# Fused decoder layer on one core: the first six hidden tiles' down projection as seven products for eight, their block sums by GpSimd, and a last plain chunk of four tiles

## The chip, the cores and the metric

The kernel runs on one core of one Trainium2 chip. The metric is the device time of one execution in microseconds. Engines are named as in the profile: PE (TensorE matmul), PEld (TensorE weight load), DVE (VectorE), ACT (ScalarE), POOL (GpSimd) and SP (SyncE, which issues most transfers). An index behind "L" is a line of the kernel before.

## The reference

The kernel computes one layer for 576 tokens (512 of a prompt, 64 of a sample group): a mixer, a cross attention and a feed-forward part. The change is in the feed-forward part and in the residual behind it:

```python
x = x + _rms(o) * g_post_x
u = _rms(x) * g_pre_ffn
f = (jax.nn.silu(u @ w_gate) * (u @ w_up)) @ w_down
x = x + _rms(f) * g_post_ffn
```

`x` is 576 x 1024, `w_gate` and `w_up` are 1024 x 2816, `w_down` is 2816 x 1024. The 2816 hidden features are 22 tiles of 128.

## The kernel before

**Layout and precision.** Everything lies with features on the partitions and the 576 tokens along the free axis. Each float32 operand is split into a high part (a cast to fp32r, by ACT) and a low part (the difference, mostly by DVE), and every product is three matmuls: high by high, high by low, low by high. `split` (L190, L191) is this pair of instructions. Tokens are cut in two in one of two ways: `HALVES` (256 and 320) for plain products, `E` (288 and 288) for the others.

**Gate and up.** Hidden tiles 0 to 3 are plain products (`half_tile`, L1693): eight input tiles by three matmuls for each half. `gated` (L1700) then applies silu (ACT, L1683) and the product with up (DVE, L1686) and writes the hidden tile's high and low parts with `hidden` (L1688) to the buffers `hh` and `hl`. Tiles 4 to 21 go in pairs, in class `Pair` (L1853), which computes a 2 x 2 block product with seven block products in place of eight. For that it needs sums and differences of the weights' blocks (`sums`, `diffs`, `parts2` to `parts4` of class `Seven`, on ACT, DVE and by accumulating transfers that POOL issues) and of the activations' blocks (`tsum`). A pair runs in three stretches. `early` has products 0 and 1, `mid` 2, 3 and 4, `late` 5 and 6. Product 2 accumulates into the same bank as product 0 (`s.x`), so it waits until ACT has copied that bank to `cc` (L1881); product 4 in turn waits until ACT has copied it to `ct` (`ev2`, L1888), and product 5 until the copy to `cc` (`ev3`, L1892). One pair's `late` is run behind the next one's `early`.

**Down.** Before, the down projection has four chunks of hidden tiles:

- tiles 0 to 3, plain (`down_chunk`, L1998, from L2066), right behind the first pair; ACT copies the results to `f2`;
- tiles 4 to 9 and 10 to 15, seven products for eight (class `Down`, L1939); DVE adds each product to `f2` (L1947). They read block sums of the hidden tiles, which `Hidden.sums` (L1928, DVE) computes from a pair's four gated blocks in `gt` before these are overwritten;
- tiles 16 to 21, plain: first the 320 tokens for all eight output tiles (L2112), then the 256 tokens, in the tail.

**The tail** (from L2117) is written out by hand: `half0` are the products of 256 tokens, `evac0` adds a bank to `f2`, squares it and scales it by the gain, `sum0` adds up the squares, `resid1` finishes the 320 tokens (norm, residual, store), `x_rows` and `x_copy` turn the residual's tiles around, and `f_rows`, `root` and `last` finish the 256 tokens.

**Order.** From L2037 on, for tiles 0 to 3 and the first pair (`pp[0]` for gate, `pp[1]` for up), and again in the tail, the order on every engine is that of a table of positions: `at_(p, step)` puts a step at position p, and the steps are traced in rising p. A unit of p is one half tile's 24 matmuls in the first table and one output tile's products in the second. In between, a scheduler orders each engine's instructions at build time. In either case every engine takes its instructions strictly in order.

Of the kernel before, what the change touches and what calls it, by code (L numbers as in the profile page):

```python
# [115 lines left out]
def build(nc, tc, ctx, I, O):  # L116
# [72 lines left out]
    def split(hi, lo, src, eng=None, cast=None):  # L189
        c = (cast or A.copy)(hi, src)  # L190
        (eng or V).tensor_tensor(lo, src, hi.bitcast(F32), op=ALU.subtract)  # L191
        return c
# [843 lines left out]
    def SL0(name, dt=F32R):  # L1036
        return big0.tile([P, KT, T], dt, name=name, tag="s0", bufs=1)
# [639 lines left out]
    at_(12.9, S.dma_start, x_d, x)  # L1677


    H = []  # L1680

    def silu(j, i):
        A.activation(ct[:, (j + i) % 2, :], B[("g", j), i], AF.Silu)  # L1683
# [2 lines left out]
        V.tensor_tensor(ct[:, (j + i) % 2, :], ct[:, (j + i) % 2, :], B[("u", j), i], op=ALU.mult)  # L1686

    def hidden(j, i):  # L1688
        if not H:
            H.extend((SL0("hh0"), SL(2, "hl0", F32R)))  # L1690
        split(H[0][:, j, E[i]], H[1][:, j, E[i]], ct[:, (j + i) % 2, :])

    def half_tile(*ms):  # L1693

# [208 lines left out]
    class Hidden:  # L1903
# [90 lines left out]
    def down_part(nk, j, i, ps, w, k0, k1):  # L1994
        t0, n = HALVES[i]
        return gemm(ps, [(*w, nk)], act(hh), act(hl), t0, n, k0, k1)

    def down_chunk(nk, order, last, w_of, evac, n1):  # L1998

        ps = {}  # L2000

        def get(j, i):
            if (j, i) not in ps:
                ps[j, i] = (GP if len(ps) < 3 or len(ps) % 2 else MP)("ps_dn")[:, :HALVES[i][1]]
            return ps[j, i]

        for n_, (j, i) in enumerate(order[:3]):
            down_part(nk, j, i, get(j, i), w_of(j), 0, n1)
            if n_ == 0:
                last.late()  # L2010
        for n_, (j, i) in enumerate(order):
            p = get(j, i)
            m = down_part(nk, j, i, p, w_of(j), n1 if n_ < 3 else 0, nk) if n_ > 2 or n1 < nk else None
            evac(n_, j, i, p, m)

    def ev_first(n_, j, i, ps, m):
        t0, n = HALVES[i]
# [12 lines left out]
    for p, n_, step in ((19.05, 0, "load"), (19.1, 1, "load"), (21.9, 0, "sums"), (22.05, 0, "high1"), (22.6, 0, "diffs"),  # L2030
                        (23.0, 0, "place3"), (23.05, 0, "parts2"), (23.9, 1, "sums"), (24.1, 0, "parts3"),
                        (23.62, 0, "parts4"), (24.48, 0, "early"), (24.97, 1, "high1"), (25.0, 0, "mid"),
                        (25.4, 1, "diffs"), (26.05, 1, "parts2"), (26.48, 1, "early"), (27.5, 0, "late"),
                        (26.45, 1, "place3"), (26.47, 1, "parts4"), (28.1, 1, "parts3"), (28.5, 1, "mid")):
        at_(p, lambda n_, step: getattr(pp[n_], step)(), n_, step)
    plan.sort()
    with tc.manual_schedule(engines={TE.engine, A.engine, V.engine, G.engine, S.engine}):  # L2037
        for p, _, fn in plan:
# [10 lines left out]
        for p, _, fn in plan:  # L2049
            if p > 19.02:  # L2050
                fn()
    hh, hl = H
    f2 = SL(4, "f_ffn")


    firsts = {}

    def w_first(j):
        if j not in firsts:
            with tc.issue_after(pp[0].ev3.ins) if j < 2 else ExitStack():  # L2060
# [12 lines left out]
    class Plain:  # L2073
# [1 line left out]
            s.b = hh, hl  # L2075

        def put(s, j, a, i, g):
            split(*[t_[:, j % 8, E[i]] for t_ in s.b], g)


    for n_, j0 in enumerate((10, 16)):
        store = stores[-1]
        last = run([lambda: Pair(j0, 0, None)] + downs(512 + 768 * n_, store), last)
        stores.append((Plain if n_ else Hidden)(SL0("hh%d" % n_), SL(2, "hl%d" % n_, F32R)))
        last = run([pair(j0, 1, stores[-1])] + [pair(j, up, stores[-1]) for j in (j0 + 2, j0 + 4) for up in range(2)], last)
# [4 lines left out]
    wdh = SL(1, "wdh", F32R, (P, 6, 768))  # L2090
    wdl = bx.tile([P, 16, 288], F32R, name="wdl", tag="b5").rearrange("p a b -> p (a b)").rearrange("p (j c) -> p j c", c=768)
    x2 = SL(3, "x2")
    ssqf = ssq_tile("ssqf")
    rb = rb_tile("pf_rb")
# [1 line left out]

    def w_of(j):
        if j not in kept:
            src = I["wdown"][j, :, 2048:2816]
            raw = fp.tile([P, 1024], F32, name="rawx", tag="rawx", bufs=2) if j % 2 else None  # L2100
            kept[j] = split_w(src, 768, 768, raw=raw, to=None if j > 5 else (wdh[:, j, :], wdl[:, j, :]))
        return kept[j]

    def down_evac(n_, j, i, ps, m):
# [40 lines left out]
    def half0(j, k):  # L2145
        if k == 0:
            tail[j] = (MP if j % 2 else GP)("ps_dn")[:, :256]
        down_part(6, j, 0, tail[j], w_of(j), k, k + 1)

    def evac0(j):  # L2150
        fj = f2[:, j, 0:256]
        V.tensor_tensor(fj, fj, tail[j], op=ALU.add)
# [10 lines left out]

    def resid1(q):
        o, c = f2[:, 2 * q:2 * q + 2, 256:T], x2[:, 2 * q:2 * q + 2, 256:T]
        V.tensor_tensor(o, o, rb[:, 256:T].unsqueeze(1).to_broadcast([P, 2, 320]), op=ALU.mult)
        V.tensor_tensor(c, c, o, op=ALU.add)
        S.dma_start(O["y1"][:, 2 * q:2 * q + 2, :], c)

    for j in range(8):  # L2170
        for k in range(6):
            at_(j + k / 6, half0, j, k)
        at_(j + 1.03, evac0, j)
        if 0 < j < 7:
            at_(j + 1.45, sum0, j)
    at_(0.99, root, "pf1", [(ssqf, 0)], HCHUNKS[1])
    at_(1.9, root_end, "pf1")
    at_(2.32, root_rows1)
    at_(2.6, lambda: A.copy(rb[:, 256:T], tail["ps"][:, 0:320]))
    for q, p in enumerate((2.95, 4.1, 5.1, 6.1)):  # L2180
        at_(p, resid1, q)

    parts = [(c, d) for c in range(2) for d in range(2)]
# [38 lines left out]
        store(3)  # L2222

    for i in range(4):
        at_(4.0 + i, x_rows, i)
        at_(4.55 + i, x_copy, i)
# [40 lines left out]
def pack(inp):  # L2267
# [37 lines left out]
    out["wup"] = _units(i["w_up"][0], KT)  # L2305

    w = _units(i["w_down"][0], NFFN)
    taken = [0, 1, 2, 3] + [j + k for j in (4, 10) for k in (0, 2, 4, 1, 3, 5)] + list(range(16, 22))
# [47 lines left out]
```

## Time and profile before

| | |
|---|---|
| median of 3 runs | 1096.13 us (1095.41 to 1097.32) |
| the profiled execution | 1096.77 us, span 1095.0 us |
| granted TensorE clock, mean | 0.998 |
| busy share of the span | PE 99%, PEld 94%, DVE 69%, ACT 56%, POOL 21% |
| matmuls | 8124 |
| bytes moved | 182.29 MB, mean 166 GB/s |

All traces are of the profiled execution; what lies around its span is 1.77 us. A row of a timeline has the start, the length, the engine, the line, the operation, the tile written and the tiles read, and the shape; in brackets stands the idle time before it and what ended it. Rows of PE overlap (matmuls are pipelined), so the price of a matmul is the distance from one start to the next.

### The profile page before, as it was taken

The numbers are of one execution on the slowest core, as the hardware profiler recorded it, in microseconds if no ns is written. First come the engines' busy times: TensorE is split into PE (matmuls) and PEld (weight loads), VectorE is DVE, ScalarE is ACT, GpSimd is POOL, SyncE is SP. The second block draws the span as 40 slices with busy tenths as digits, with TensorE's granted clock in tenths as the row PEclk, the third lists the DMA queues.
The fourth block names the chain that finished last, engine by engine and source line by source line (L and its number), as shares of the span: only waits on it lengthen the run. The fifth ranks groups of instructions, "written<-read, shape, count | busy, mean of one in ns | idle before, by whom it ended". The sixth has DMA issues, their size and how long they took to land.

```text
span 1095.0 us, 20715 instructions
## 1 busy us (share of the span) xinstructions
PE 1084.1 (99%) x8124; PEld 1027.5 (94%) x8124; DVE 754.0 (69%) x1507; ACT 611.7 (56%) x1098; POOL 225.8 (21%) x305
## 2 busy tenths in 40 slices
PE   9999999999999999999999999999999999999997
PEld 8999887778999999999988879999999999999997
DVE  6896785658877775558744546676566877787555
ACT  7767632455654555656545445645566566656653
POOL 1332643313213112000144301100011121111000
PEclk9999999999999999999999999999999999999999
DMA  6785635435655349653467775644386687588532
GB/s 204 170 154 127 170 111 174 163 84 177 189 149 146 106 132 312 205 189 102 150 215 271 264 248 163 217 161 109 104 195 142 150 196 173 116 188 186 128 130 88
DMA packets 58967, 182.29 MB, mean 166 GB/s; under 512 B 6605, under 2 KB 11853, under 8 KB 58357
## 3 DMA queue, kind: packets, MB, share of 16 engines
q1 hardware_dynamic: 42740, 138.06, 39.0%
q0 software_dynamic: 15552, 41.95, 19.8%
q8 instruction: 64, 1.05, 0.4%
q10 hardware_dynamic: 576, 0.95, 0.3%
q14 instruction: 35, 0.28, 0.1%
HBM read 160.28 MB, written 20.65 MB: 165 GB/s over the span
## 4 chain that ended last, share of the span: by engine, by line
PE 88%; DVE 5%; ACT 4%; DMA 2%; issue 1%; SPq 0%; POOL 0%; DVEq 0%; ACTq 0%
PE ps_v L814 5%; PE ps_in L202 4%; PE ps_in L201 4%; PE ps_in L204 4%; PE ps_o L202 3%; PE ps_o L204 3%; PE ps_o L201 3%; PE ps_g L1848 3%; PE ps_g L1849 3%; PE ps_g L1850 3%; PE ps_u L1848 3%; PE ps_u L1850 3%; PE ps_u L1849 3%; PE ps_dn L1848 2%; PE ps_dn L1849 2%; PE ps_dn L202 2%
## 5 line engine op out<-in xcount | busy, mean ns | idle before, releaser
L201 PE MATMUL ps_in<-uh,whi 128*128 128x320 f32 (+1 forms) x544 | 164.0, 302 | 0.4 <-DVE cb L450 0.4
L204 PE MATMUL ps_in<-uh,wlo 128*128 128x320 f32 (+1 forms) x544 | 163.2, 300 | 0.0
L202 PE MATMUL ps_in<-ul,whi 128*128 128x320 f32 (+1 forms) x544 | 162.7, 299 | 0.0
L179 ACT CAST whi<-raw 128x1024 fp32r<-128x1024 f32 (+1 forms) x104 | 105.2, 1013 | 96.2 <-PE ps_in L202 26.1
L186 DVE TENSOR_TENSOR wlo<-raw,whi 128x512 fp32r<-128x512 f32 (+1 forms) x96 | 96.6, 1009 | 66.5 <-ACT whi L179 65.8
L201 PEld LDWEIGHTS ps_in<-uh,whi 128*128 128x128 f32 x544 | 103.1, 190 | 3.4 <-issue 1.7
L204 PEld LDWEIGHTS ps_in<-uh,wlo 128*128 128x128 f32 x544 | 103.0, 190 | 1.2 <-issue 0.4
L202 PEld LDWEIGHTS ps_in<-ul,whi 128*128 128x128 f32 x544 | 103.1, 190 | 0.6
L184 POOL DMA_DIRECT2D wlo<-win x32 | 27.9, 871 | 80.1 <-ACT wlo L183 72.0
L1848 PE MATMUL ps_g<-b,whi 128*128 128x288 f32 x144 | 42.5, 295 | 0.0
L1849 PE MATMUL ps_g<-b,whi 128*128 128x288 f32 x144 | 42.4, 295 | 0.0
L1848 PE MATMUL ps_u<-b,whi 128*128 128x288 f32 x144 | 42.4, 295 | 0.0
L1849 PE MATMUL ps_u<-b,whi 128*128 128x288 f32 x144 | 42.4, 295 | 0.0
L1821 ACT CAST whi<-rawx 128x1024 fp32r<-128x1024 f32 (+1 forms) x26 | 25.7, 987 | 27.8 <-PE ps_dn L1849 13.8
L191 DVE TENSOR_TENSOR wlo<-sw,whi 128x1024 fp32r<-128x1024 f32 (+1 forms) x26 | 29.6, 1140 | 14.9 <-ACT whi L190 14.7
L201 PE MATMUL ps_xo<-qh,whi 128*128 128x288 f32 x128 | 38.5, 302 | 0.2 <-ACT whi L179 0.2
L202 PE MATMUL ps_o<-mixs_l,whi 128*128 128x320 f32 (+1 forms) x128 | 38.2, 299 | 0.0
L204 PE MATMUL ps_o<-mixm_h,wlo 128*128 128x256 f32 (+1 forms) x128 | 38.2, 298 | 0.0
L202 PE MATMUL ps_o<-mixm_l,whi 128*128 128x256 f32 (+1 forms) x128 | 37.9, 296 | 0.0
L201 PE MATMUL ps_xq<-u2h,whi 128*128 128x320 f32 (+1 forms) x128 | 37.9, 300 | 0.0
L201 PE MATMUL ps_o<-mixm_h,whi 128*128 128x256 f32 (+1 forms) x128 | 37.9, 296 | 0.0
L204 PE MATMUL ps_xq<-u2h,wlo 128*128 128x320 f32 (+1 forms) x128 | 37.9, 296 | 0.0
(765 smaller groups left out, 3838.9 us busy)
## 6 DMA issues: line engine op xcount, KB each, us to landing
raw<-win SPq DMA_DIRECT2D x35, 512.0 KB, 3.9
raw<-wout SPq DMA_DIRECT2D x17, 512.0 KB, 3.6
raw<-wxq SPq DMA_DIRECT2D x13, 512.0 KB, 3.6
raw<-wgate SPq DMA_DIRECT2D x13, 512.0 KB, 3.5
raw<-wup SPq DMA_DIRECT2D x13, 512.0 KB, 5.3
wlo<-win POOLq DMA_DIRECT2D x24, 256.0 KB, 5.1
kva<-kc SPq DMA_DIRECT2D x12, 512.0 KB, 5.7
kva<-vc SPq DMA_DIRECT2D x12, 512.0 KB, 6.0
```

The costliest lines, as they stand in the source:

```text
L179: casts.append(A.copy(hi[:, :n], raw[:, :n]))
L184: G.dma_start(lo[:, a:b], src[:, a:b], accum_op=ALU.add)
L186: e.tensor_tensor(lo[:, a:b], raw[:, a:b], hi[:, a:b].bitcast(F32), op=ALU.subtract)
L191: (eng or V).tensor_tensor(lo, src, hi.bitcast(F32), op=ALU.subtract)
L201: mm(ps, wh, ah, start=i == 0, stop=False)
L202: mm(ps, wh, al, start=False, stop=False)
L204: m = mm(ps, tiles[order[c]][1], xh(order[c], t0, n), start=False, stop=c == len(tiles) - 1)
L814: mm(ps, a, b, skip_group_check=True, **kw)
L1821: A.copy(s.h3[:, s.all], s.r2[:, s.all])
L1848: mm(ps, wh, b[0][k], start=start and k == 0, stop=False, skip_group_check=True)
L1849: mm(ps, wh, b[1][k], start=False, stop=False, skip_group_check=True)
L1850: m = mm(ps, wl, b[0][k], start=False, stop=k == nk - 1, skip_group_check=True)
```

## The change

Tiles 0 to 3 are no longer projected by themselves. The pairs' chunks become tiles 0 to 5, 6 to 11 and 12 to 17, all with `Down`, and the plain last chunk keeps tiles 18 to 21. The order of the tiles in the packed weight follows.

`Down` needs block sums of tiles 0 and 1, and of 2 and 3. The gated blocks of these tiles come one by one, and only their high and low parts are kept (the blocks that `Down` doesn't read go to `te`). So `single_sums` computes each pair's four sums out of the parts, with ten tensor-tensor instructions on POOL into `gt`, and `single_parts` splits them (a cast of 1152 columns on ACT, a difference on DVE). The positions of these four steps in the first table are new. In the first chunk, ACT copies a product to `f2` where it is the first one. The tail's positions are new, and in it POOL scales output tiles 0 to 5 and does one of the four residuals.

```diff
     def hidden(j, i):
-        split(H[0][:, j, E[i]], H[1][:, j, E[i]], ct[:, (j + i) % 2, :])
+        split(*stores[0].single(j, i), ct[:, (j + i) % 2, :])
...
+        def single(s, j, i):
+            if (j % 2, i) == (0, 1):
+                return [s.rest()[:, j + e, :] for e in range(2)]
+            return s.place(j // 2, {(0, 0): 4, (1, 0): 5, (1, 1): 6}[j % 2, i])
+
+        def single_sums(s, q):
+            g, b = gates(4 + 2 * q), [[[t_.bitcast(F32) for t_ in s.single(2 * q + a, i)] for i in range(2)] for a in range(2)]
+            for out, steps_ in ((g[0][0], ((b[0][1][0], b[0][0][0], 0), (None, b[0][1][1], 1), (None, b[0][0][1], 0))),
+                                (g[0][1], ((b[1][1][0], b[0][1][0], 0), (None, b[1][1][1], 1), (None, b[0][1][1], 0))),
+                                (g[1][1], ((b[1][1][0], g[0][0], 0), (None, b[1][1][1], 1))),
+                                (g[1][0], ((b[1][0][0], g[1][1], 0), (None, b[1][0][1], 1)))):
+                for x_, y_, add in steps_:
+                    G.tensor_tensor(out, out if x_ is None else x_, y_, op=ALU.add if add else ALU.subtract)
+
+        def single_parts(s, q):
+            k = 4 * q
+            split(*[t_[:, (8, 0)[q]:(8, 0)[q] + 4, :] for t_ in s.b], gt[:, k:k + 4, :])
...
         def add(s, a, i, ps):
             o = f2[:, s.j + a, E[i]]
-            V.tensor_tensor(o, o, ps, op=ALU.add)
+            if (s.j, a, i) in begun:
+                V.tensor_tensor(o, o, ps, op=ALU.add)
+            else:
+                begun.add((s.j, a, i))
+                A.copy(o, ps)
...
+    for q, p, d in ((0, 22.4, 24.45), (1, 24.61, 26.46)):
+        at_(p, lambda q: stores[0].single_sums(q), q)
+        at_(d, lambda q: stores[0].single_parts(q), q)
...
-    down_chunk(4, [(j, i) for j in range(8) for i in (1, 0)], pp[1], w_first, ev_first, 4)
     seq.extend(pp)
-    last = run([pair(j, up, stores[0]) for j in (6, 8) for up in range(2)], None)
+    last = pp[1]
...
-    for n_, j0 in enumerate((10, 16)):
+    for n_, j0 in enumerate((6, 12, 18)):
         store = stores[-1]
-        last = run([lambda: Pair(j0, 0, None)] + downs(512 + 768 * n_, store), last)
+        last = run([pair(j0, 0, store)] + downs(768 * n_, store), last)
...
-    down_chunk(6, [(j, 1) for j in (6, 7, 0, 1, 2, 3, 4, 5)], last, w_of, down_evac, 4)
+    down_chunk(4, [(j, 1) for j in (6, 7, 0, 1, 2, 3, 4, 5)], last, w_of, down_evac, 2)
...
-        if j < 7:
+        if j < 6:
+            G.tensor_scalar(fj, fj, PAR("g_postffn", j), None, op0=ALU.mult)
+        elif j < 7:
             A.activation(fj, fj, AF.Copy, scale=PAR("g_postffn", j))
...
     def resid1(q):
...
+        e = G if q == 0 else V
+        e.tensor_tensor(o, o, rb[:, 256:T].unsqueeze(1).to_broadcast([P, 2, 320]), op=ALU.mult)
+        e.tensor_tensor(c, c, o, op=ALU.add)
...
-    for q, p in enumerate((2.95, 4.1, 5.1, 6.1)):
+    for q, p in ((1, 4.2), (0, 4.21), (2, 5.3), (3, 6.3)):
         at_(p, resid1, q)
...
-        at_(4.0 + i, x_rows, i)
+        at_((0.6, 2.5, 4.5, 6.0)[i], x_rows, i)
```

How this moves instructions is shown at three places, as a comparison of the two orders (- is before, + is now, no sign is both).

ACT, at the first pair's gate (`pp[0]`): `te<-ct` is the cast of the last single block (tile 2, second half), `hh<-gt` of 1152 columns the cast in `single_parts(0)`, `cc<-ps_g` the copy that product 2 waits for, `ct<-ps_g` (L1888) the one that product 4 waits for.

```order
+L190 CAST te<-ct 128x288
+L190 CAST hh_8385<-gt 128x1152
 L1881 COPY cc<-ps_g 128x288
 L1868 ACTIVATE gt<-gt 128x288
 L1800 CAST whi<-raw 128x1024
+L1795 ACTIVATE wacc<-raw 128x1024
 L1888 COPY ct<-ps_g 128x288
```

The cast of `gt`, which reads what POOL wrote, now stands ahead of the copy for product 2, and a weight step of the pair of tiles 6 and 7 (`wacc<-raw`) ahead of the copy for product 4.

DVE, at the first pair's up (`pp[1]`): `hl<-gt` of 1152 columns is the difference of `single_parts(1)`, `d_9036` and the rows that write `sw` and `rawx` are weight steps of tiles 6 and 7, `ct<-ps_u,cc` (L1872) and `gt<-gt,ct` (L1874) evacuate `pp[1]`.

```order
+L191 TENSOR_TENSOR hl_8386<-gt,hh_8385 128x1152
+L1804 TENSOR_TENSOR sw<-sw,raw 128x512
+L1811 TENSOR_TENSOR rawx<-raw,rawx 128x512
+L191 TENSOR_TENSOR wlo<-d_8897,u3h 128x512
+L1872 TENSOR_TENSOR ct<-ps_u,cc 128x288
+L1814 TENSOR_TENSOR d_9036<-raw,sw 128x512
+L1874 TENSOR_TENSOR gt<-gt,ct 128x288
+L191 TENSOR_TENSOR wlo<-d_9036,u3h 128x512
 L191 TENSOR_TENSOR hl_8386<-gt,hh_8385 128x288
 L1867 TENSOR_TENSOR gt<-ps_g,ct 128x288
```

Before, the pair of tiles 6 and 7 came a down chunk later, and none of its weight steps stood among these rows.

POOL, at the end of the program: `L2169` are the gains of output tiles 0 to 5, `L2181` and `L2182` the residual of output tiles 0 and 1.

```order
 L1107 MEMSET ssqf 128x64
-L2351 UNCONDITIONAL_BRANCH
-L2351 ISA
+L2169 TENSOR_SCALAR f_ffn<-f_ffn,par 128x256 x4
+L2181 TENSOR_TENSOR f_ffn<-f_ffn,pf_rb 128x2x320
+L2182 TENSOR_TENSOR x_12278<-x_12278,f_ffn 128x2x320
+L2169 TENSOR_SCALAR f_ffn<-f_ffn,par 128x256 x2
```

Before, POOL had nothing to do in the tail; now it has eight instructions there.

More of the change, by code (lines that the diff above doesn't have):

```diff
@@ L2003, in get @@
             if (j, i) not in ps:
-                ps[j, i] = (GP if len(ps) < 3 or len(ps) % 2 else MP)("ps_dn")[:, :HALVES[i][1]]
+                ps[j, i] = (GP if len(ps) < 3 or len(ps) % 2 == 0 else MP)("ps_dn")[:, :HALVES[i][1]]
             return ps[j, i]
-        for n_, (j, i) in enumerate(order[:3]):
+        for n_, (j, i) in enumerate(order[:4]):
             down_part(nk, j, i, get(j, i), w_of(j), 0, n1)
@@ L2077, in put @@
         def put(s, j, a, i, g):
[L2078 to L2081 removed]
+            split(*[t_[:, j - 18, E[i]] for t_ in s.b], g)
+    for n_, j0 in enumerate((6, 12, 18)):
         store = stores[-1]
[L2083 to L2085 removed]
+        last = run([pair(j0, 0, store)] + downs(768 * n_, store), last)
+        stores.append((Plain if n_ == 2 else Hidden)(SL0("hh%d" % n_), SL(2, "hl%d" % n_, F32R)))
+        last = run([pair(j0, 1, stores[-1])] + [pair(j, up, stores[-1]) for j in range(j0 + 2, min(j0 + 6, NFFN), 2)
+                                                for up in range(2)], last)
     hh, hl = stores[-1].b
@@ L2147, in half0 @@
             tail[j] = (MP if j % 2 else GP)("ps_dn")[:, :256]
[L2148 removed]
+        down_part(4, j, 0, tail[j], w_of(j), k, k + 1)
     def evac0(j):
@@ L2165, in resid1 @@
         o, c = f2[:, 2 * q:2 * q + 2, 256:T], x2[:, 2 * q:2 * q + 2, 256:T]
-        V.tensor_tensor(o, o, rb[:, 256:T].unsqueeze(1).to_broadcast([P, 2, 320]), op=ALU.mult)
-        V.tensor_tensor(c, c, o, op=ALU.add)
+        e = G if q == 0 else V
+        e.tensor_tensor(o, o, rb[:, 256:T].unsqueeze(1).to_broadcast([P, 2, 320]), op=ALU.mult)
+        e.tensor_tensor(c, c, o, op=ALU.add)
         S.dma_start(O["y1"][:, 2 * q:2 * q + 2, :], c)
     for j in range(8):
-        for k in range(6):
-            at_(j + k / 6, half0, j, k)
+        for k in range(4):
+            at_(j + k / 4, half0, j, k)
         at_(j + 1.03, evac0, j)
@@ L2175, in build @@
             at_(j + 1.45, sum0, j)
[L2176 to L2179, printed above, removed]
-    for q, p in enumerate((2.95, 4.1, 5.1, 6.1)):
+    at_(1.45, root, "pf1", [(ssqf, 0)], HCHUNKS[1])
+    at_(2.8, root_end, "pf1")
+    at_(3.4, root_rows1)
+    at_(3.75, lambda: A.copy(rb[:, 256:T], tail["ps"][:, 0:320]))
+    for q, p in ((1, 4.2), (0, 4.21), (2, 5.3), (3, 6.3)):
         at_(p, resid1, q)
@@ L2307, in pack @@
     w = _units(i["w_down"][0], NFFN)
-    taken = [0, 1, 2, 3] + [j + k for j in (4, 10) for k in (0, 2, 4, 1, 3, 5)] + list(range(16, 22))
+    taken = [j + k for j in (0, 6, 12) for k in (0, 2, 4, 1, 3, 5)] + list(range(18, 22))
     out["wdown"] = np.ascontiguousarray(w.reshape(8, P, NFFN, P)[:, :, taken].reshape(w.shape))
```

40 lines of the change are left out of this document (14 added, 26 removed).

## The prediction

> **What bounds the kernel now.** I read the page first, then the busy time by stage, then the engines' timelines where the change sits. The page's busy times:
>
> ```profile
> PE 1084.1 (99%) x8124; PEld 1027.5 (94%) x8124; DVE 754.0 (69%) x1507; ACT 611.7 (56%) x1098; POOL 225.8 (21%) x305
> ```
>
> Two stages (start:end, length, busy time and instructions of PE, PEld, DVE, ACT and POOL, granted clock, DMA share, GB/s):
>
> ```profile
> 740.00:750.00 10.00, 10.00 (x77) 10.00 (x76) 8.42 (x13) 6.91 (x11) 0.86 (x1) 1.00 0.53 93
> 840.00:880.00 40.00, 39.95 (x302) 39.71 (x301) 33.10 (x69) 21.77 (x38) 6.91 (x8) 1.00 0.68 151
> ```
>
> PE is the bound in both, at full clock. So a matmul less is time less, and whatever makes PE wait is time more. But where the block sums go (740 to 750), DVE is 84% busy too.
>
> **The matmuls saved.** The price of a matmul is the distance between starts. Here are the first and the last of twelve in a row for 288, 320 and 256 columns:
>
> ```profile
> 749.88 0.29 PE L1848 MATMUL ps_g<-u3h,whi 128*128 128x288 f32 x1
> 751.33 0.29 PE L1850 MATMUL ps_g<-u3h,wacc 128*128 128x288 f32 x1
> ...
> 785.05 0.31 PE L201 MATMUL ps_dn<-hh,whi 128*128 128x320 f32 x1
> 786.66 0.31 PE L204 MATMUL ps_dn<-hh,wlo 128*128 128x320 f32 x1
> 786.81 0.28 PE L201 MATMUL ps_dn<-hh,whi 128*128 128x256 f32 x1
> 788.12 0.28 PE L204 MATMUL ps_dn<-hh,wlo 128*128 128x256 f32 x1
> ```
>
> That is 1.45/11 = 0.132, 1.61/11 = 0.146 and 1.31/11 = 0.119 us. Six tiles leave the plain chunks: 8 outputs x 6 tiles x 3 = 144 matmuls of 320 and 144 of 256 columns, 21.0 + 17.1 = 38.2 us. Four more `Down` steps come: 4 x 7 products x 3 tiles x 3 = 252 of 288 columns, 33.3 us. **Saved: 4.9 us**, of which 48 x 0.119 = 5.7 in the tail. The first chunk's copies on ACT stand in for the 16 copies of the old first chunk and cost nothing: PE has no wait in the stages that are run like this (840 to 880: 39.95 of 40).
>
> **The block sums, and whom they hold up.** POOL's prices for a tensor-tensor of two full inputs, and two pairs of rows in which it meets DVE:
>
> ```profile
> L191 POOL TENSOR_TENSOR mk<-mko,mk 128x256 fp32r<-128x256 f32 x6 | 4.4, 743 | 0.0
> L658 POOL TENSOR_TENSOR xs<-xs,ec 128x384 f32<-128x384 f32 x8 | 8.1, 1016 | 38.4 <-DVE ec L656 38.4
> ...
> 602.65 1.29 POOL L186 TENSOR_TENSOR wlo<-raw,whi 128x512 fp32r<-128x512 f32 x1
> 602.93 1.55 DVE L186 TENSOR_TENSOR wlo<-raw,whi 128x512 fp32r<-128x512 f32 x1
> ...
> 547.98 0.69 DVE L186 TENSOR_TENSOR wlo<-raw,whi 128x512 fp32r<-128x512 f32 x1 [2.06 <-ACT whi L179]
> 548.03 1.80 POOL L186 TENSOR_TENSOR wlo<-raw,whi 128x512 fp32r<-128x512 f32 x1 [1.28 <-ACT whi L179]
> ```
>
> Between 743 (256) and 1016 ns (384), a sum of 288 columns takes 0.81 us. The other rows say more: the DVE instruction, 0.69 us by itself, took 1.55 and ended 0.54 after POOL's; POOL's, 1.29 by itself, took 1.80 and ended 1.16 after DVE's. They ran one after the other, whoever came first. So a queued sum adds about 0.81 - 0.13 = 0.68 us to a busy DVE.
>
> [...]
>
> What DVE, ACT and PE do there before:
>
> ```profile
> 746.61 0.45 DVE L191 TENSOR_TENSOR hl<-ct,hh 128x288 fp32r<-128x288 f32 x1
> 751.25 0.69 DVE L1822 TENSOR_TENSOR u3l<-rawx,whi 128x512 fp32r<-128x512 f32 x1
> 751.85 0.45 DVE L1686 TENSOR_TENSOR ct<-ct,ps_u 128x288 f32<-128x288 f32 x1
> ...
> 745.45 0.44 ACT L190 CAST hh<-ct 128x288 fp32r<-128x288 f32 x1 [0.86 <-DVE ct L1686]
> 752.33 0.43 ACT L190 CAST hh<-ct 128x288 fp32r<-128x288 f32 x1 [1.33 <-DVE ct L1686]
> 752.67 0.39 ACT L1881 COPY cc<-ps_g 128x288 f32<-128x288 f32 x1
> 754.15 1.04 ACT L1800 CAST whi<-raw 128x1024 fp32r<-128x1024 f32 x1
> 755.09 0.39 ACT L1888 COPY ct<-ps_g 128x288 f32<-128x288 f32 x1
> ...
> 753.11 0.40 PE L1848 MATMUL ps_g<-b,whi 128*128 128x288 f32 x1
> ...
> 779.57 1.16 ACT L190 CAST hh<-gt 128x1152 fp32r<-128x1152 f32 x1
> 780.76 1.36 DVE L191 TENSOR_TENSOR hl<-gt,hh 128x1152 fp32r<-128x1152 f32 x1 [0.63 <-ACT hh L190]
> ```
>
> Product 2 of `pp[0]` (753.11) starts 0.05 after the copy of its bank (752.67 + 0.39): there is no slack. That copy stands behind the cast at 752.33, this behind DVE's product at 751.85, and DVE runs without a gap from 746.61 to there.
>
> Step 1. Three of the first ten sums use blocks that are there early. The fourth needs the cast at 745.45, so seven fall where DVE is busy with two-input instructions. Interleaved, they take 7 x 0.68 = 4.8 us of it; DVE's product, the cast and the copy move by that. Then comes the new cast of 1152 columns ahead of the copy, 1.16 less the overlap of 0.1. **PE waits 4.8 + 1.0 = 5.8 us.** If DVE went first throughout, the cast would wait for POOL instead, as long. Bounds: 1.1 (the cast alone) and 6.7 (0.81 for each).
>
> Step 2. From the end of that cast to the copy for product 4 (L1888), ACT and DVE now do in turn: the low part 1.36, the add and silu (288 columns each, 0.45 as in the rows above), `whi` 1.04, the new `wacc` of the same shape 1.04 and the copy 0.39, each less some 0.05 of overlap: 4.4 us. PE is there after 0.35 for the first copy and 24 x 0.132 = 3.2 for products 2 and 3. **It waits 0.9 us** (0.5 to 1.6, if a sum of the second ten gets ahead of the low part).
>
> Step 3. The second sums start at the last single's cast. Seven run while DVE waits for `pp[0]`; a weight transfer's issue and the last three follow among DVE's weight steps, and end about 5 us after product 4 does (764.6 in this count; sums done at 769.7). ACT then has the cast of 1152, `u3h` (512 columns, 0.6, between the casts of 288 and 1024) and the copy for `pp[1]`'s product 2: done 7.1 after product 4, whereas PE needs it after four products, 6.4. From there to `pp[1]`'s product 4 these stood before:
>
> ```profile
> 761.46 0.39 ACT L1881 COPY cc<-ps_u 128x288 f32<-128x288 f32 x1
> ...
> 766.49 0.39 ACT L1888 COPY ct<-ps_u 128x288 f32<-128x288 f32 x1
> ```
>
> 5.0 us between the two copies. DVE, which held the low part back until the cast came, now has in between: that 1.36, four weight steps of 512 columns before L1874 and one behind it (0.60 from start to start, 751.25 to 751.85), L1872, L1874, a 288 low part and L1867 (0.37 each): 5.8, of which 0.85 passes before the first copy ends. With the hand-overs to ACT in between (0.4), silu, `whi` and the copy (1.9) I count 7.2 us from copy to copy, and PE has 3.2 us of work. **It waits 0.7 and 4.0; I take 4.0 for both, since the count is good to some 0.7.** Bounds: 2.4 (sums done in time) and 5.
>
> Behind `pp[1]` the next steps' weights come in time by the same count: PE's wait has given every transfer 10 us more.
>
> **The tail.** DVE's rows there (engine, operation, count: least, median and most ns; below them the last evacuation):
>
> ```profile
> L2152 DVE TENSOR_TENSOR f_ffn<-f_ffn,ps_dn x8: 392/422/422, 1068.1 to 1086.2; 128x256 f32<-128x256 f32 x8
> L2166 DVE TENSOR_TENSOR f_ffn<-f_ffn,pf_rb x4: 818/820/826, 1071.8 to 1080.5; 128x640 f32<-128x640 f32 x4
> L2167 DVE TENSOR_TENSOR x<-x,f_ffn x4: 824/824/826, 1072.7 to 1081.3; 128x640 f32<-128x640 f32 x4
> ...
> 1086.15 0.42 DVE L2152 TENSOR_TENSOR f_ffn<-f_ffn,ps_dn 128x256 f32<-128x256 f32 x1 [2.13 <-PE ps_dn L204]
> ```
>
> Before, an output tile has 18 x 0.119 = 2.1 us of PE, and DVE idles 2.13 us ahead of the last evacuation. Now it is 12 x 0.119 = 1.4 us, and from output tile 3 on DVE still has three residuals of 1.6, five evacuations and four sums of 0.37: 8.1 us, where PE has four tiles, 5.7. That is up to 2.4 behind, less what the transposes between them add to PE. POOL's residual of 640 columns (two instructions, 1.5 us each by the rate from 256 to 384 columns) and two gains (0.74 at most, as for two inputs; 0.5 taken) shut DVE's two-input work out for some 3.5. So the last evacuation comes 0.5 us (no POOL, transposes that take most of the 2.4) to 4 us behind PE. I take **3.0**, as POOL's part is sure. PE gives back half of the 5.7 it saved there.
>
> **The sum.** Against the profiled execution: 1096.8 - 4.9 + 5.8 + 0.9 + 4.0 + 3.0 = 1105.6. The median stands 0.64 below that execution, so 1104.9; I say **1104.8 us**. With the terms' lower bounds that don't need POOL beside DVE (4.6, 0.5, 2.4, 0.5) it is 1099, with the upper ones (6.7, 1.6, 5, 4) 1108.5.
>
> **The rivals.**
>
> *POOL beside DVE.* If 288-column sums don't hold up DVE, the first ten end about 751.5, ahead of the cast. What is left are the insertions: 1.1 + 0.9 + 2.4 + 0.5 = 4.9, as much as is saved: 1096.1, no change. For it: the rows of exclusion have 512 columns. Against it: all of them, both ways round.
>
> *Faster.* The saving comes through: ACT gets to the new cast after its sums are done, and the insertions fall into gaps of PE that I can't see. It decides at 752.7, when the single's cast ends: sums done by then, and a copy for product 4 not behind it, give 1096.1 - 4.9 = 1091.2, with the tail's wait 1092. For it: seven sums of 0.81 from 745.9 end at 751.6. Against: DVE has no gap there, and product 2 has no slack.
>
> *Slower still.* Each sum waits for the one before it by semaphore. If a handover costs 0.2 us in which DVE starts its next instruction, and ten more of the sums so meet DVE's long ones (1.36), steps 1 and 3 grow by 17 x 0.2: 1108, and up to 1111.
>
> **Chances.** Forecast 0.71, POOL beside DVE 0.11, faster 0.08, slower still 0.10. About 0.2% (2.2 us) can be told from no change. The second case spreads over both sides (0.02 faster, 0.07 same, 0.02 slower): faster 0.10, same 0.07, slower 0.83. The range leaves out the faster case and half of the slowest: 1096.5 to 1109.5. The forecast's own is 1099 to 1108.5.
>
> **What would show it.** Right: `PE L1848` waits some 6 us for ACT at `pp[0]`'s product 2 and 4 us at `pp[1]`'s product 4; DVE's 512-column steps stretch from 0.69 to about 1.4 beside L1942; the last evacuation has no idle time ahead of it. Wrong: L1942 done by 752 with DVE at its old pace, or PE without a gap from 750 to 790; then the time is at or under 1096.

## The result, and the profile after

| | before | after |
|---|---|---|
| median | 1096.04 us (1095.19 to 1097.32, 5 runs) | 1108.87 us (1107.80 to 1109.10, 5 runs) |
| ratio, 95% interval | | 1.0115 (1.010 to 1.013) |
| the profiled execution | 1096.77, span 1095.0 | 1108.19, span 1106.4 |
| granted clock, mean | 0.998 | 0.993 |
| matmuls | 8124 | 8088 |

The change is slower by 12.8 us, with 36 matmuls fewer. Lines of POOL, DVE and ACT in this part are those of the changed kernel.

The page's busy times, PE's waits from 700 us on (who waits, for whom; in total, times, longest), and five stages around the block sums (columns as in the prediction):

```profile
PE 1084.2 (98%) x8088; PEld 1027.0 (93%) x8088; DVE 775.3 (70%) x1543; ACT 620.1 (56%) x1110; POOL 263.7 (24%) x341
```

```profile
PE ps_g L1848 <- ACT cc L1881: 5.1, 1, 5.1
PE ps_u L1848 <- ACT ct L1888: 2.9, 1, 2.9
PE ps_xt L2205 <- ACT raw L2214: 1.7, 1, 1.7
PE ps_ft L2205 <- ACT f_ffn L2171: 1.6, 1, 1.6
PE ps_dn L201 <- ACT hh L190: 0.6, 1, 0.6
PE ps_u L1848 <- ACT cc L1892: 0.5, 1, 0.5
```

```profile
740.00:752.00 12.00, 12.00 (x92) 12.00 (x91) 10.97 (x13) 7.38 (x11) 6.32 (x5) 1.00 0.33 84
752.00:757.40 5.40, 0.31 (x4) 0.08 (x2) 4.27 (x6) 1.78 (x3) 4.51 (x6) 0.94 0.23 28
757.40:763.60 6.20, 6.20 (x26) 6.20 (x27) 1.49 (x2) 2.62 (x4) 5.96 (x7) 0.50 0.36 102
763.60:774.40 10.80, 10.80 (x83) 10.80 (x83) 8.38 (x13) 5.47 (x10) 4.63 (x6) 1.00 0.59 114
777.60:781.00 3.40, 3.40 (x15) 3.40 (x16) 1.58 (x2) 2.73 (x4) 0.54 (x1) 0.55 0.59 181
```

PE is called busy for the whole of 757.4 to 763.6, but it starts 26 matmuls there, where 6.2 us at 0.132 hold 47. The granted clock is 0.50, and again 0.55 from 777.6. Both stretches follow a wait.

The timeline of all engines where the first wait arises:

```profile
746.92 1.12 POOL L1942 TENSOR_TENSOR gt<-gt,hl 128x288 f32<-128x288 f32 x1 [0.46 <-DVE hl L191]
747.30 1.29 DVE L1814 TENSOR_TENSOR d<-raw,sw 128x512 f32<-128x512 f32 x1
748.12 1.14 POOL L1942 TENSOR_TENSOR gt<-gt,te 128x288 f32<-128x288 f32 x1
748.51 1.83 DVE L191 TENSOR_TENSOR wlo<-sw,whi 128x1024 fp32r<-128x1024 f32 x1
...
755.08 0.44 DVE L1686 TENSOR_TENSOR ct<-ct,ps_u 128x288 f32<-128x288 f32 x1
755.55 0.43 ACT L190 CAST te<-ct 128x288 fp32r<-128x288 f32 x1 [5.00 <-DVE ct L1686]
755.89 1.15 ACT L190 CAST hh<-gt 128x1152 fp32r<-128x1152 f32 x1
756.94 0.39 ACT L1881 COPY cc<-ps_g 128x288 f32<-128x288 f32 x1
757.38 0.61 PE L1848 MATMUL ps_g<-b,whi 128*128 128x288 f32 x1 [5.09 <-ACT cc L1881]
757.79 0.44 PE L1849 MATMUL ps_g<-b,whi 128*128 128x288 f32 x1
758.03 0.44 PE L1850 MATMUL ps_g<-b,wlo 128*128 128x288 f32 x1
```

POOL's sums and DVE's steps end in turn: from L1814 on, a DVE step of 512 columns takes 1.16 to 1.29 for 0.69. The chain to PE is as forecast: DVE's product, the single's cast, the cast of 1152 columns, the copy, PE. Behind the wait, a matmul starts every 0.24 us.

In the tail, beside POOL's residual (timeline), and the last evacuation:

```profile
1088.40 1.69 POOL L2181 TENSOR_TENSOR f_ffn<-f_ffn,pf_rb 128x640 f32<-128x640 f32 x1
1088.59 1.79 DVE L2176 TENSOR_TENSOR ssqf<-ssqf,sq 128x256 f32<-128x256 f32 x1
1090.18 1.60 POOL L2182 TENSOR_TENSOR x<-x,f_ffn 128x640 f32<-128x640 f32 x1
1090.31 0.41 DVE L2164 TENSOR_TENSOR f_ffn<-f_ffn,ps_dn 128x256 f32<-128x256 f32 x1
1090.63 1.82 DVE L2181 TENSOR_TENSOR f_ffn<-f_ffn,pf_rb 128x640 f32<-128x640 f32 x1
...
1097.44 0.41 DVE L2164 TENSOR_TENSOR f_ffn<-f_ffn,ps_dn 128x256 f32<-128x256 f32 x1
```

DVE's sum and multiplication with two SBUF inputs wait out POOL's here (1.79 for 0.42 and 1.82 for 0.82); the evacuation, whose second input is in PSUM, does not (0.41). PE's two waits of 1.7 and 1.6 above lie in the tail too: the copy and the gain that it waits for stand on ACT behind squares that wait for DVE's evacuations.

**Where the time went.** I cut both spans at three starts on PE: `pp[0]`'s product 0, the first product behind `pp[1]`'s product 4, and the tail's first matmul of 256 columns. Single executions differ by 1 to 2 us as wholes, so the intervals say more than the totals.

| interval | before | after | difference | forecast |
|---|---|---|---|---|
| to `pp[0]`'s product 0 | 749.88 | 748.98 | -0.90 | 0 |
| to the end of `pp[1]`'s product 4 | 19.25 | 31.65 | +12.40 | +10.7 |
| to the tail's first 256 columns | 295.81 | 297.80 | +1.99 | +0.8 |
| to the end of the span | 30.06 | 27.97 | -2.09 | -2.7 |
| span | 1095.0 | 1106.4 | +11.40 | +8.8 |

The -0.90 lies ahead of everything that the change moves on PE; the changed kernel's variants below reach the same product between 747.9 and 750.3.

### The profile page after: what moved, and what is told of

Read it like the earlier page. It is cut to its first block, busy times and chain, and to the rows that moved or that the text cites. A ratio compares the mean times of both kernels' runs of the same rounds, so it can differ in the third digit from the quotient of the medians.

```text
span 1106.4 us, 20772 instructions
## 1 busy us (share of the span) xinstructions
PE 1084.2 (98%) x8088; PEld 1027.0 (93%) x8088; DVE 775.3 (70%) x1543; ACT 620.1 (56%) x1110; POOL 263.7 (24%) x341
## 4 chain that ended last, share of the span: by engine, by line
PE 83%; DVE 8%; ACT 3%; issue 3%; DMA 2%; POOL 0%; DVEq 0%; SPq 0%; ACTq 0%; POOLq 0%
PE ps_in L202 4%; PE ps_in L201 4%; PE ps_in L204 4%; PE ps_v L814 3%; PE ps_o L202 3%; PE ps_o L204 3%; PE ps_o L201 3%; PE ps_dn L1848 3%; PE ps_dn L1849 3%; PE ps_dn L1850 3%; PE ps_g L1848 3%; PE ps_g L1850 3%; PE ps_g L1849 3%; PE ps_u L1848 3%; PE ps_u L1849 3%; PE ps_u L1850 3%
## 5 line engine op out<-in xcount | busy, mean ns | idle before, releaser
L179 ACT CAST whi<-raw 128x1024 fp32r<-128x1024 f32 x95 | 99.3, 1047 | 90.4 <-PE ps_in L202 26.4
L186 DVE TENSOR_TENSOR wlo<-raw,whi 128x1024 fp32r<-128x1024 f32 (+1 forms) x87 | 88.9, 1025 | 62.1 <-ACT whi L179 59.2
L1849 PE MATMUL ps_dn<-hl,whi 128*128 128x288 f32 x168 | 49.3, 295 | 0.0
L1848 PE MATMUL ps_dn<-hh,whi 128*128 128x288 f32 x168 | 48.9, 296 | 0.1
L1848 PE MATMUL ps_g<-b,whi 128*128 128x288 f32 x144 | 43.9, 305 | 5.1 <-ACT cc L1881 5.1
L1821 ACT CAST whi<-rawx 128x1024 fp32r<-128x1024 f32 (+1 forms) x30 | 28.9, 965 | 31.3 <-PE ps_dn L1849 17.6
L1849 PE MATMUL ps_g<-b,whi 128*128 128x288 f32 x144 | 43.7, 303 | 0.0
L1970 DVE TENSOR_TENSOR f_ffn<-f_ffn,ps_dn 128x288 f32<-128x288 f32 x68 | 30.0, 450 | 16.9 <-PE ps_dn L1850 14.7
L191 DVE TENSOR_TENSOR wlo<-sw,whi 128x1024 fp32r<-128x1024 f32 (+1 forms) x30 | 34.0, 1135 | 9.2 <-ACT whi L190 9.1
L1800 ACT CAST whi<-raw 128x1024 fp32r<-128x1024 f32 (+1 forms) x30 | 28.9, 963 | 17.4 <-PE ps_dn L1849 8.3
```

The lines of the kernel that those rows point to most:

```text
L179: casts.append(A.copy(hi[:, :n], raw[:, :n]))
L186: e.tensor_tensor(lo[:, a:b], raw[:, a:b], hi[:, a:b].bitcast(F32), op=ALU.subtract)
L1800: s.c1 = A.copy(s.h1[:, s.all], s.r1[:, s.all])
L1848: mm(ps, wh, b[0][k], start=start and k == 0, stop=False, skip_group_check=True)
L1849: mm(ps, wh, b[1][k], start=False, stop=False, skip_group_check=True)
```

## The experiments

Each is an edit of the changed kernel, and an index in its rows is a line of its own kernel. "First interval" is that from `pp[0]`'s product 0 to the end of `pp[1]`'s product 4 (before 19.25, after 31.65). The excess is the median over the kernel before in the same series; the change's own is 12.8.

**1. PE kept busy (warm).** Matmuls without a reader fill the two waits.

```diff
...
         def mid(s):
+            warm(pp[0:1] == [s], 38)
             s.mul(s.x, 2, tsum[2], False)
...
+            warm(pp[1:2] == [s], 23)
             s.mul(s.x, 4, tsum[3], False)
```

> PE fills its two waits with matmuls that nobody reads: 38 of 288 columns ahead of pp[0]'s product 2 (38 x 0.132 = 5.0 us, the wait was 5.1) and 23 ahead of pp[1]'s product 4 (3.0, the wait was 2.9). Theory (the half-speed cadence of 0.24 us behind each wait comes of PE's idling): the cadence stays at 0.13, granted clock 1.00 from 750 to 785, and 1.4 us (the second stretch alone, if DVE and ACT set the time of product 4 of pp[1] by themselves) to 4.3 us (both) come back: 1104.6 to 1107.5. Rival (the clock falls for another reason, such as the contention of DVE and POOL): 0.24 us again behind the same places, and no gain: 1108.9.

Measured: 1106.0 us, ratio 1.0098 (1.0083 to 1.0113), excess 10.2; first interval 29.6. PE's waits and the stage behind the first of them:

```profile
PE ps_g L1848 <- ACT ct L1895: 0.9, 1, 0.9
...
PE ps_u L1848 <- ACT ct L1895: 0.5, 1, 0.5
```

```profile
757.40:763.60 6.20, 5.32 (x38) 5.08 (x39) 1.44 (x2) 2.63 (x5) 5.96 (x7) 1.00 0.36 103
```

The clock stays at 1.00: the half speed came of PE's idling, not of what DVE and POOL did (POOL is as busy here, 5.96). Of the 4.2 us that the slow stretches cost, the first interval gives back 2.1. Most of the rest shows as two new waits for L1895 (L1888 in the changed kernel): 0.9 at `pp[0]`'s product 4, which the slow stretch had covered, and 0.5 at `pp[1]`'s.

**2. The sums on DVE (dve_sums).**

```diff
-                    G.tensor_tensor(out, out if x_ is None else x_, y_, op=ALU.add if add else ALU.subtract)
+                    V.tensor_tensor(out, out if x_ is None else x_, y_, op=ALU.add if add else ALU.subtract)
```

> The twenty sums go to DVE, all else is the change's. Theory (POOL's sums shut DVE out, 1.2 us from one to the next with a DVE instruction between, 0.68 more each than DVE alone): on DVE a sum costs 0.37, so seven take 2.6 in place of 4.8, and the wait at pp[0]'s product 2 falls from 5.1 to about 3.3; its half-speed stretch shrinks with it; the second ten now lie on DVE too, which gives some back at pp[1]: 1105 to 1108. Rival (POOL runs beside DVE, and the wait comes of the cast's place alone): DVE only gets 7.4 us more work: 1110 or more, with a wait of over 5 us.

Measured: 1107.31 us, ratio 1.0108 (1.0093 to 1.0123), excess 11.5; first interval 29.8. The wait at product 2, DVE's first and last sum of the first ten:

```profile
PE ps_g L1848 <- ACT cc L1881: 5.5, 1, 5.5
```

```profile
746.03 0.45 DVE L1942 TENSOR_TENSOR gt<-te,hh 128x288 f32<-128x288 f32 x1
746.52 0.46 DVE L1942 TENSOR_TENSOR gt<-gt,te 128x288 f32<-128x288 f32 x1
...
750.21 0.46 DVE L1942 TENSOR_TENSOR gt<-gt,hl 128x288 f32<-128x288 f32 x1
```

My figure for the wait was wrong, and a wait of over 5 us is the sign that I had given the rival. The rows decide against it: without sums on POOL, DVE's steps of 512 columns are back at 0.68 or 0.69. On DVE all ten stand behind one another in the busy stretch, the three early ones too, and a sum that reads the one before it starts 0.49 after it, not 0.37: ten take 4.6 us, where seven on POOL stretch DVE by some 0.6 each, 4.2. So a sum on POOL takes no less from a busy DVE (0.6) than a sum of DVE's own (0.46), and the place is as bad for either. The shorter interval comes of less half speed: 15 slow matmuls in place of 35.

**3. Sums and casts behind the copies (late_sums).** `sg` is a buffer of its own for the sums; POOL's queue begins with the pair that needs the last single block.

```diff
...
-    for q, p, d in ((0, 22.4, 24.45), (1, 24.61, 26.46)):
+    for q, p, d in ((1, 24.4, 26.5), (0, 24.41, 28.6)):
```

> The sums have a buffer of their own, POOL does the second ten first (they need the last single block, so none runs before 752), and both casts of 1152 columns come behind the copies for pp[0]'s product 2. Theory (first ten sums in DVE's way, then the cast ahead of the copy): the wait of 5.1 at product 2 goes, and its half-speed stretch (2.9) with it: 8 us. All twenty sums then meet DVE's weight steps of pp[0], pp[1] and tiles 6 and 7, at 0.68 each 13.6 us, of which DVE had some 10 free; so 2 to 6 us may come back as waits of pp[1] or of the first Down step: 1101 to 1107. Rival (PE waits for ACT's and DVE's other new work there): a wait of over 2 us stays at product 2.

Measured: 1106.79 us, ratio 1.0106 (1.0089 to 1.0123), excess 11.0; first interval 29.2. PE's waits for ACT:

```profile
PE ps_u L1848 <- ACT ct L1888: 8.1, 1, 8.1
```

Product 2 no longer waits at all, which confirms its cause: the sums and the cast ahead of the copy, moved together here. But thirteen of the twenty sums on POOL then hold DVE up from 757 to 773 (its steps of 512 columns take 0.91 to 1.96 there, for 0.69), and the wait is back at `pp[1]`'s product 4, as one of 8.1 us. Moving POOL's sums moves the wait.

**4. The tail without POOL (tail_no_pool).**

```diff
-        if j < 6:
-            G.tensor_scalar(fj, fj, PAR("g_postffn", j), None, op0=ALU.mult)
-        elif j < 7:
+        if j < 7:
             A.activation(fj, fj, AF.Copy, scale=PAR("g_postffn", j))
...
-        e = G if q == 0 else V
+        e = V
```

> POOL has nothing in the tail: its six gains go back to ACT and its residual to DVE. Theory (POOL shuts DVE out there): DVE's stretched rows (1.79 for a sum of 0.42, 1.82 for a multiplication of 0.82) go, 2.4 us, and DVE gets 1.7 for the fourth residual: 0.7 us less, 1108.2. Rival (POOL works beside DVE): 1.7 us more, 1110.6.

Measured: 1107.54 us (1106.48 to 1110.22), ratio 1.0113 (1.0098 to 1.0128), excess 11.7. The last interval is 27.24 in place of 27.97: 0.7 less, as expected. What POOL took over it had held up elsewhere.

**5. Weight buffers of their own (own_weights).**

```diff
-            kept[j] = split_w(src, 512, 512, raw=raw, to=(wdh[:, j, :], wdl[:, j, :]))
+            kept[j] = split_w(src, 512, 512, raw=raw, to=None if j > 5 else (wdh[:, j, :], wdl[:, j, :]))
```

> The last chunk's output tiles 6 and 7 get weight buffers of their own again, as before the change, in place of wdh and wdl, which come free only when the last pair has ended. Theory (the 2.0 us that the change loses between pp[1] and the tail are 0.85 of matmuls and 1.2 of waits at the last pair's end, 0.7 ahead of product 5 and 0.8 at a hidden tile's cast, because no product of the last chunk could be put between): the waits go, 1.2 us less: 1107.4. Rival (the waits come of the last pair's own evacuation): the same 1108.6.

Measured: 1108.24 us, ratio 1.0107 (1.0092 to 1.0122), excess 12.2. The interval up to the tail falls from 297.80 to 297.04. The wait at product 5 (0.5 in the changed kernel's waits) is gone, since products of the last chunk fill it; the one at the hidden tile's cast stays (0.7). So 0.8 of the 1.2 us come of the buffers.

**6. The tail's row from PSUM (tail_psum).** With the gains on ACT, as in experiment 4:

```diff
...
-        e = G if q == 0 else V
-        e.tensor_tensor(o, o, rb[:, 256:T].unsqueeze(1).to_broadcast([P, 2, 320]), op=ALU.mult)
-        e.tensor_tensor(c, c, o, op=ALU.add)
+        V.tensor_tensor(o, o, tail["ps"][:, 0:320].unsqueeze(1).to_broadcast([P, 2, 320]), op=ALU.mult)
+        (G if q == 0 else V).tensor_tensor(c, c, o, op=ALU.add)
...
-    at_(3.75, lambda: A.copy(rb[:, 256:T], tail["ps"][:, 0:320]))
```

> In the tail the residual's multiplication (DVE) reads the norm's row from PSUM, where PE wrote it, and not its copy in SBUF; POOL has one of the four residual additions and nothing else; gains on ACT. Theory (POOL shuts out only DVE instructions with two SBUF inputs): multiplications and evacuations run at 0.82 and 0.42 beside POOL's addition, DVE does 0.82 less than with nothing on POOL, and the row comes 0.4 earlier: 1 to 2 us under the run without POOL in the tail (1107.5): 1105.5 to 1106.5. Rival (POOL shuts out any DVE instruction): rows of 1.4 to 1.8 us beside POOL's addition, and 1107.5 to 1108.5.

Measured: 1107.75 us (1104.81 to 1108.00), ratio 1.0097 (1.0082 to 1.0112), excess 11.7; the last interval is 26.29, 0.95 under experiment 4. Beside POOL's addition:

```profile
1088.10 1.55 POOL L2179 TENSOR_TENSOR x<-x,f_ffn 128x640 f32<-128x640 f32 x1 [29.07 <-DVE f_ffn L2178]
1088.12 0.41 DVE L2164 TENSOR_TENSOR f_ffn<-f_ffn,ps_dn 128x256 f32<-128x256 f32 x1
1088.45 0.81 DVE L2178 TENSOR_TENSOR f_ffn<-f_ffn,ps_rb 128x640 f32<-128x640 f32 x1
1089.30 1.04 DVE L2179 TENSOR_TENSOR x<-x,f_ffn 128x640 f32<-128x640 f32 x1
```

With the row in PSUM the multiplication runs at 0.81 beside POOL, where the changed kernel's took 1.82 (1090.63 above); the addition of two SBUF tiles still waits for POOL's end (1.04 for 0.82; it ends 0.69 after POOL's). So beside POOL's addition both DVE instructions with an input in PSUM, the evacuation (0.41) and the multiplication (0.81), keep their pace, and the one with two SBUF inputs does not. The median lies in the rival's range, but the medians don't tell this run from experiment 4: the executions of each scatter over 3 us. The rows and the interval are what shows it.

**7. The sums where DVE is idle (sums_in_gap).**

```diff
...
+    PS = (((22.4, G, slice(0, 3)), (24.7, V, slice(3, 10))), ((24.72, V, slice(0, 4)), (28.2, V, slice(4, 10))))
+    for q, p, d in ((0, 22.4, 25.5), (1, 24.72, 28.6)):
...
+                    p.behind, p.late_dve = p.behind + [pp[0].ev2], True
```

(`late_dve` puts the DVE steps of tiles 6 and 7 behind `pp[0]`'s last evacuation.)

> The sums lie where DVE was idle: the three first on POOL at their old place, seven of the first ten and four of the second on DVE between pp[0]'s first evacuation and the one behind product 4 (11 x 0.37 = 4.1 us, a gap of 5.0), six behind pp[1]'s weight steps; the casts of 1152 behind the copies that PE waits for; weight steps of tiles 6 and 7 behind pp[0]'s last evacuation. The sums have a buffer of their own. Theory (both waits come of what stands ahead on DVE and ACT, and each brings a half-speed stretch): of the 12.4 us lost there some 11 come back, no half-speed stretch is left: 1096 to 1100. Rival (DVE has no room for the sums anywhere, so the wait only moves, as with the sums behind the copies on POOL): a wait of 3 us or more at pp[1] or at the first Down step, 1103 or more.

Measured: 1101.1 us, ratio 1.0042 (1.0027 to 1.0057), excess 5.0, a little above what I expected. A wait of 1.8 is left at product 2, and no slow stretch. POOL's three first sums now wait for the new buffer and meet DVE (timeline):

```profile
PE ps_g L1849 <- ACT cc L1882: 1.8, 1, 1.8
```

```profile
745.52 0.88 POOL L1947 TENSOR_TENSOR sg<-te,hh 128x288 f32<-128x288 f32 x1 [9.02 <-DVE b L1749]
745.66 1.30 DVE L1811 TENSOR_TENSOR rawx<-raw,rawx 128x512 f32<-128x512 f32 x1
746.49 1.14 POOL L1947 TENSOR_TENSOR sg<-sg,te 128x288 f32<-128x288 f32 x1
746.88 1.29 DVE L1814 TENSOR_TENSOR d<-raw,sw 128x512 f32<-128x512 f32 x1
...
748.09 1.83 DVE L191 TENSOR_TENSOR wlo<-sw,whi 128x1024 fp32r<-128x1024 f32 x1
```

Three sums, three steps stretched by 0.6 each (1.30 for 0.68, 1.29 for 0.68, 1.83 for 1.22): 1.8 us, the whole of the wait. It is the cleanest measure of the price: 0.6 us of DVE for a sum of 288 columns.

**8. Edits 5, 6 and 7 together (all_three).**

> The three edits before this one together (sums in DVE's gap, own weight buffers, the tail's row read from PSUM). Theory: they lie in three places and add up, 1108.6 - 11 - 1.2 - 2.5 = 1093.9, 0.2% under the kernel before; 1093 to 1097. Rival (what is gained at one place is lost as a wait at the next): over 1098.

Measured: 1098.09 us (10 runs), ratio 1.0016 (1.0006 to 1.0026), excess 2.0. That is above my range and where I had put the rival, but the rival's mechanism is not what happened: singly the edits gave 7.8, 0.6 and 1.1 us, 9.5 together, and here they give 10.8. My sum was too low because I had put 11 for edit 7 alone.

**9. The three sums back at their early place (gap_early).** The first pair's sums stand in `gt` again, in its second half.

> As all_three, but the first pair's sums stand in gt again (in the half that the pair of tiles 6 and 7 uses), so that POOL's three first sums need not wait for the buffer that the activations' block sums still read, and run where DVE is idle, ahead of 740. Theory (those three, beside DVE's weight steps, are the whole of the remaining wait at product 2: 3 x 0.6 = 1.8 us): that wait goes, 1098.1 - 1.8 = 1096.3, the time of the kernel before. Rival (PE also waits there for DVE's or ACT's other work): over 1 us of wait stays, and 1097 or more.

Measured: 1095.44 us (11 runs), ratio 0.9997 (0.9988 to 1.0006). The wait at product 2 is gone. PE's largest waits from 700 us on:

```profile
PE ps_xt L2213 <- ACT raw L2222: 1.3, 1, 1.3
PE ps_dn L201 <- ACT hh L190: 0.5, 1, 0.5
PE ps_u L1849 <- ACT ct L1889: 0.4, 1, 0.4
PE ps_g L1849 <- ACT whi L1800: 0.4, 1, 0.4
```

**10. Two attempts on the tail (gap_tail, tail_terms).**

```diff
-        (G if q == 0 else V).tensor_tensor(c, c, o, op=ALU.add)
+        (G if q < 2 else V).tensor_tensor(c, c, o, op=ALU.add)
...
-        at_((1.35, 3.1, 5.1, 6.6)[i], x_copy, i)
+        at_((1.35, 3.1, 4.95, 6.6)[i], x_copy, i)
```

> As gap_early, and in the tail POOL does two of the residual's additions, and the copy of the residual's third turned block stands ahead of the square that waits for DVE, so that PE need not wait for that copy (1.3 us). Theory (PE is the bound of the tail again once it doesn't wait for that copy): the last evacuation comes 0.8 to 1.5 us earlier: 1094.8 to 1095.5, under the kernel before. Rival (DVE still is the bound, and POOL's second addition costs as much as it takes over): the time of gap_early.

Measured: 1095.35 us (11 runs), ratio 0.9996 (0.9987 to 1.0004). PE's wait of 1.3 for the copy went, and one of 1.7 for the gain of output tile 6 came, because DVE is still late: a square's sum beside the addition that POOL took on lasted 1.44 for 0.42. The last interval is 26.45, against 26.33 in gap_early.

The second attempt, on top of it, gives the sums of the squares of output tiles 3 to 6 to PE:

```diff
...
-        if 0 < j < 7:
+        if 0 < j < 3:
             at_(j + 1.45, sum0, j)
+        if 3 <= j < 7:
+            at_(j + 1.99, term, j)
...
```

> As gap_tail, and the squares of output tiles 3 to 6 are not added up by DVE (four sums of 0.34) but taken by PE as further terms of the tiny matmuls (128x1) that add up over the partitions, in PE's gaps of the tail. Theory (DVE is the bound of the tail, from the first residual to the last evacuation): 4 x 0.34 = 1.4 us less on DVE, of which PE's wait for a square takes some back: 0.7 to 1.2 us under gap_tail, 1094.2 to 1094.7, and 0.1% under the kernel before. Rival (PE or ACT is the bound there): the time of gap_tail, 1095.4.

Measured: 1095.68 us (11 runs), ratio 0.9998 (0.9989 to 1.0007). The last evacuation (timeline) now waits for PE:

```profile
1081.01 0.50 PE L2193 MATMUL ps_ss<-c,sq 128*128 128x1 f32 x4
...
1083.96 0.42 DVE L2176 TENSOR_TENSOR f_ffn<-f_ffn,ps_dn 128x256 f32<-128x256 f32 x1 [1.83 <-PE ps_dn L204]
```

The tiny matmuls are recorded as groups of four, and four such groups came ahead of it. From the start of each to the next start on PE it is 0.36 to 0.44 us, 1.5 in all: PE took on what DVE gave (1.4). No version here beats the kernel before by more than can be told; the best three equal it.

## Why the prediction was right, and where its terms were off

Forecast 1104.8 (1096.5 to 1109.5, slower 0.83), measured 1108.87. The direction and its mechanism held, but the time lies 4 us above the forecast and just above the forecast's own range (1108.5). That it is no further off is partly luck: 4.2 us that I had left out met waits that came to 8.2 us where I had counted 10.7. The steps:

- **The matmuls saved.** 36 fewer, as counted. But the part ahead of the tail is a cost of 0.8, not a gain, and the tail gives 5.7; the sum had that right.
- **Step 1** (5.8 us at product 2): 5.2 from start to start. Seven interleaved sums, then the cast, as worked out, but a sum takes 0.6 and not 0.68. Experiment 3 shows that it goes with their place, 7 and 9 that each sum takes 0.6 from DVE.
- **What followed step 1 was left out.** I priced PE's wait as a wait alone. It also halved PE's clock: 24 matmuls at 0.24 behind a first one at 0.41, 2.8 us; and 1.4 us more behind the second wait. These 4.2 us are the largest error. Experiment 1 shows the cause. The granted clock is 0.50 in both stretches, and a matmul starts every 0.24 us there, every 0.13 behind them. The clock was at half for 6.8 and 3.4 us, and the first 0.6 and 0.3 us of that still lay in the waits.
- **Step 2** (0.9 at product 4): no wait in the trace, because the slow stretch covered it; 0.9 in experiment 1, where PE ran at full speed. The count was right, and worth nothing here.
- **Step 3** (4.0 in all, 0.7 of it at `pp[1]`'s product 2): nothing at product 2, 3.0 at product 4. The same cover explains 0.7 of it: in experiment 1, with PE at full speed, it is 3.7 from product 3's last start to product 4's first, less one matmul. Product 2 doesn't wait there either. My count had the second sums done 5 us after `pp[0]`'s product 4; they were done 3.9 after it in experiment 1 and 1.6 after it in the changed kernel.
- **Behind `pp[1]`** I had only the matmuls' 0.8; it was 2.0. Experiment 5 names two thirds of the rest: the last chunk's first two output tiles lost buffers of their own, so nothing could be put between the last pair's products. That line of the diff I hadn't priced.
- **The tail** (5.7 less, 3.0 back): 3.6 back. The last evacuation had no idle time ahead of it. POOL's part in it is 0.7 (experiment 4), where I had taken POOL's 3.5 for the sure part; so the term is near for a reason other than mine. That DVE is shut out for the length of a gain on POOL, as those 3.5 have it, no run shows: in the changed kernel a gain takes 0.92 or 0.93 alone, and DVE's additions beside one take 0.98 or 0.99 for 0.82 (timeline, 1087.67, 1092.49 and 1094.91). Of the 2.9 that stay without POOL, experiment 6 takes off 0.95 by making DVE's work shorter. When DVE gives up 1.4 more (experiment 10, second attempt), PE takes on as much and the interval stays; how much of the last 2 us is DVE's alone is not shown.

Of the rivals, *POOL beside DVE* falls: every row above has them in turn, except where DVE's second input is in PSUM. *Faster* needed the sums done by 752.7; they ended at 754.6, though this kernel is 0.9 earlier at `pp[0]`'s product 0. *Slower still* had the right size (1108 to 1111) by the wrong mechanism: the handover between sums is 0.1, and no extra DVE step came in between.

## What to carry to other kernels

The sums given to GpSimd were not off VectorE's books where VectorE was busy with instructions of two SBUF inputs: each took 0.6 us from it. Price such work at what it takes from VectorE there, and look for a stretch where VectorE is idle, or for an input that can stay in PSUM (the multiplication beside GpSimd took 0.81 us so, and 1.82 with both inputs in SBUF). A wait of TensorE is not priced by its length alone: here 1.4 us at half speed followed one of 2.9, 2.8 us one of 5.1, and nothing one of 1.8. When a wait is removed or covered, ask what it had been hiding, and where the work that caused it will stand instead.

## What was not expected of the hardware

The half-speed stretch does not follow the length of the wait. Waits at `pp[0]`'s product 2 of 5.1 us were followed by 24 slow matmuls in the changed kernel and by 18 in tail_psum; one of 5.5 by 15 in dve_sums. At `pp[1]`'s product 4, a wait of 8.1 in late_sums was followed by 18 and one of 2.9 in the changed kernel by 11, but waits of 3.2 in tail_psum and 2.7 in dve_sums by none at half clock.

The granted clock shows why. In the changed kernel it is half from 756.76 to 763.59 and from 777.24 to 780.66, for 6.83 and 3.42 us, with 13.65 at full clock between: its changes lie on a grid of 3.41 us, two windows of it, four and then one. Here are the windows of this grid around the wait of 2.9 in the changed kernel, and around the wait of 3.2 in tail_psum (columns as in the prediction, the clock is the third number from the end):

```profile
773.83:777.24 3.41, 0.90 (x7) 0.66 (x5) 1.67 (x4) 2.55 (x6) 0.00 (x0) 1.00 0.46 77
777.24:780.66 3.42, 3.08 (x13) 3.08 (x14) 1.89 (x2) 2.93 (x4) 0.20 (x1) 0.50 0.49 141
780.66:784.07 3.41, 3.41 (x28) 3.41 (x27) 2.90 (x8) 1.05 (x4) 0.66 (x1) 1.00 0.86 182
...
772.23:775.65 3.42, 1.62 (x13) 1.38 (x11) 2.74 (x6) 1.59 (x4) 0.24 (x1) 1.00 0.49 77
775.65:779.06 3.41, 2.02 (x14) 1.89 (x15) 0.83 (x2) 3.41 (x6) 0.00 (x0) 1.00 0.18 19
779.06:782.50 3.44, 3.44 (x29) 3.44 (x28) 2.76 (x5) 0.86 (x2) 0.85 (x1) 1.00 0.80 238
```

The wait of 2.9 lies mostly in one window: PE is busy for 0.90 of its 3.41 us, and the next window has half the clock. The longer wait of 3.2 is cut by an edge, PE is busy for 1.62 and 2.02 us of two windows, and the clock stays. The six traces with such waits and a half-speed stretch (the changed kernel, dve_sums, late_sums, tail_no_pool, own_weights, tail_psum) agree. Around these waits, in these six, half clock followed every full-speed window in which PE was idle for 0.71 of it or more, and none with 0.53 or less. Full clock came back behind a window with 0.16 or less idle, and not behind one with 0.18 or more. So a wait of 2.9 us, shorter than a window of the grid, halved the clock here.
